# The second branch's merge gates of row pairs two and three by seven block products, with h of those rows kept transposed in DRAM

## The chip, the cores and the metric

The kernel runs on one core of one Trainium2 chip. The metric is device time in microseconds (us) of one execution. Three runs of the kernel before took 2771.01, 2769.5 and 2768.42 us, median 2769.5. One further execution was taken with the hardware profiler.

The engines are called by their short names: PE (TensorE, matmuls), DVE (VectorE), ACT (ScalarE), POOL (GpSimd) and SP (SyncE, which here only issues transfers).

## The reference

One layer of a streaming encoder, for 2048 prompt rows and 64 decode rows, all in float32, width 1024:

```python
h = rmsnorm(x, norm_g)
q, k, v, ga, u, gb, mg = split(h @ w_in)        # 1024 columns each, mg has 2048
att = stick_breaking(q, k, v)                   # 8 heads of 128, causal
pb = multi_scale_pool(u, w_pool, pool_scale)
y_a = (att * silu(ga)) @ w_br_a
y_b = (pb * silu(gb)) @ w_br_b
gate = sigmoid(mg)
m = gate[..., :1024] * y_a + gate[..., 1024:] * y_b
y = rmsnorm(x + m @ w_out, final_g)
```

The change is about the second half of `mg`, the 1024 columns of `w_in` from 7168 on, and `gate[..., 1024:]`, which I call the second branch's merge gate. k, v and the tail of u are outputs too.

## The kernel before

**Number format.** Every matmul operand is split into a rounded high part and the remainder (`split`, lines 76 to 82: ACT casts, DVE or POOL subtracts). A product is three matmuls: high by high, high by low, low by high.

**Two halves.** The 2112 rows are worked in two halves, A (1024 prompt rows and the 64 decode rows, `RA` = 1088) and B (1024 rows). For each half the transposed h is built first: rows are loaded, normalised (`normalise`, lines 197 to 205: DVE scales, POOL multiplies by the gain for the right half of the columns), transposed by PE and split into `hhi` and `hlo` (`transposed_h`, lines 207 to 214). Then come the eight attention heads with their projections, then the gates and the pooling branch.

**Direct slabs.** `proj` (lines 276 to 290) makes 128 output columns: it loads a slab of `w_in`, splits it, and runs for each column group of rows 8 k-tiles by 3 matmuls. The groups of half A are 512, 256 and 320 rows wide, those of half B 512 and 512. `merge_gate` is a slab whose result goes through a sigmoid to DRAM (`sm_d`), through one of three buffers with the tag "out" (`outgoing`), which key and value rows use as well. On half A the slabs are interleaved with the attention of the decode rows (`sample_stream`); `run` gives each generator a total time and always takes the one that is least far along, so these totals set PE's order.

**Closing stage.** y_a, y_b and m @ w_out are made by block products (Winograd's form of Strassen's scheme): rows in pairs of 352-row blocks, columns and depth in halves of 512, seven products instead of eight. A pair covers 704 rows, so three pairs cover all 2112. `order` lists the products: branch, pair t, product p. One product is 2 x 2 output tiles of 12 matmuls (`product`, lines 986 to 994), 48 matmuls of 352 columns. The weight side needs four differences of weight blocks per weight matrix (`differences`), kept in DRAM (`tw_d`): those of w_br_a and w_br_b are made by POOL (`weight_sums`) while half B's last merge gates run, those of w_out by DVE in the closing stage (`sums_step`). `forms` loads and splits a weight block, in two halves. The row side is loaded by `load_rows` from the transposed branch inputs in DRAM (`aT_d`, `bT_d`), combined by `sum3`, `sum12`, `sum4` and split by `make`, two products ahead. `emit` takes a finished block: DVE adds the kept product, multiplies by the gate, for the second branch adds the first branch's part, and POOL's queue stores it.

**What sets the order.** PE follows the program throughout. In the closing stage PE, DVE, ACT and SP all follow the program, in which `weights_at(2 * s + cc)` is called twice per product; `when` and `sums_at` say at which of these half products a weight form or a difference is made. The other engines' order before that is set by a scheduler. In all stages an engine's queue is worked in order, SP's too: a transfer that waits for its buffer holds those behind it.

## Time and profile before

| | |
|---|---|
| timed runs, median of 3 | 2769.5 us (2768.42 to 2771.01) |
| profiled execution, whole | 2771.89 us |
| its span | 2770.2 us |
| granted PE clock, mean | 0.995 |
| half A, up to the last transposes of half B's h | about 0 to 1130 us |
| half B's heads and pooling | to about 2090 us |
| half B's last 15 merge gate slabs | to 2257 us |
| first 42 block products | 2257 to about 2580 us |
| output product, residual, norm | to the end |

A profile row has the line, the engine, the operation, the names of output and input, the shape and a count, then busy time and mean duration, then the idle time of the engine just before and what ended it. Window rows have the busy time of each engine in a stretch with the number of instructions in brackets. Waits have the total, how often, and the longest. PE's matmuls overlap, so their pace is read from their starts or from a count per window and not from their durations.

### The profile page before, as it was taken

How to read it: one execution, taken by the hardware profiler on the slowest of the kernel's cores; microseconds unless marked ns; L12 is line 12 of the kernel's file. 1: busy time of each engine (PE TensorE's matmuls, PEld its weight loads, DVE VectorE, ACT ScalarE, POOL GpSimd, SP SyncE). 2: the span in 40 equal slices, each digit the busy share in tenths (PEclk: the TensorE clock that was granted, in tenths of full speed). 3: DMA queues.
4: the chain of work that ended last, by engine and by line, in shares of the span. 5: the costliest groups of instructions: out<-in, count | busy, mean ns of one | idle time of the engine just before them, and what ended most of it. 6: DMA issues, size and time to landing. Idle time of an engine off the chain costs nothing.

```text
span 2770.2 us, 41810 instructions
## 1 busy us (share of the span) xinstructions
PE 2703.7 (98%) x15052; PEld 2362.0 (85%) x15052; DVE 1833.7 (66%) x2843; ACT 1267.0 (46%) x2520; POOL 582.7 (21%) x1285
## 2 busy tenths in 40 slices
PE   6999999999999999999999999999999999999898
PEld 6988888988998989888888888887778889999786
DVE  6555555567777684487878888886452237786776
ACT  4445444455555553355555555554222223333343
POOL 2112222220000001222432343331005501110001
PEclk9999999999999999999999999999999999999999
DMA  5224222234544545311111211112337848777653
GB/s 147 79 84 131 73 72 72 77 96 152 153 155 146 157 141 153 94 46 54 54 46 50 58 54 42 51 38 84 111 100 227 268 162 275 268 258 239 219 161 118
DMA packets 344397, 343.87 MB, mean 124 GB/s; under 512 B 30062, under 2 KB 286558, under 8 KB 344188
## 3 DMA queue, kind: packets, MB, share of 16 engines
q1 hardware_dynamic: 329756, 294.26, 34.4%
q0 software_dynamic: 14432, 46.93, 4.8%
q8 instruction: 118, 1.93, 0.3%
q14 instruction: 91, 0.75, 0.1%
HBM read 232.46 MB, written 108.65 MB: 123 GB/s over the span
## 4 chain that ended last, share of the span: by engine, by line
PE 89%; DVE 5%; DMA 2%; issue 2%; ACT 1%; POOL 1%; SPq 0%; POOLq 0%; DVEq 0%; ACTq 0%
PE pj L284 17%; PE pj L285 17%; PE pj L286 17%; PE tr L638 4%; PE x L989 3%; PE x L991 3%; PE x L993 3%; PE att L655 2%; PE att L654 2%; PE z L627 2%; PE att L653 2%; PE z L626 2%; PE z L625 2%; PE y L989 2%; PE y L991 2%; PE y L993 2%
## 5 line engine op out<-in xcount | busy, mean ns | idle before, releaser
L284 PE MATMUL pj<-hhi,whi 128*128 128x512 f32 (+2 forms) x2608 | 946.3, 363 | 0.0
L286 PE MATMUL pj<-hhi,wlo 128*128 128x512 f32 (+2 forms) x2608 | 918.4, 352 | 0.0
L285 PE MATMUL pj<-hlo,whi 128*128 128x512 f32 (+2 forms) x2608 | 917.5, 352 | 0.1
L286 PEld LDWEIGHTS pj<-hhi,wlo 128*128 128x128 f32 x2608 | 492.4, 189 | 65.1
L284 PEld LDWEIGHTS pj<-hhi,whi 128*128 128x128 f32 x2608 | 495.0, 190 | 59.6 <-ACT hhi L81 0.2
L285 PEld LDWEIGHTS pj<-hlo,whi 128*128 128x128 f32 x2608 | 494.1, 189 | 59.1 <-DVE hlo L82 0.4
L579 DVE TENSOR_TENSOR_SCAN om<-om 128x513 f32<-128x513 f32 (+3 forms) x356 | 387.4, 1088 | 212.3 <-POOL om L561 108.4
L569 ACT ACTIVATE om<-z 128x512 f32<-128x512 f32 (+2 forms) x320 | 171.6, 536 | 322.1 <-PE z L627 271.6
L82 DVE TENSOR_TENSOR wlo<-raw,whi 128x512 fp32r<-128x512 f32 x248 | 176.9, 717 | 197.9 <-ACT whi L81 197.2
L581 POOL COPY carry<-om 128x1 f32<-128x1 f32 x356 | 78.6, 221 | 918.3 <-DVE om L579 877.8
L582 DVE TENSOR_TENSOR be<-be,om 128x512 f32<-128x512 f32 (+3 forms) x356 | 230.2, 647 | 31.5
L81 ACT CAST whi<-raw 128x512 fp32r<-128x512 f32 x256 | 158.3, 623 | 184.2 <-PE pj L285 167.9
L81 ACT CAST a<-tr 128x512 fp32r<-128x512 f32 (+2 forms) x356 | 188.0, 528 | 100.6 <-PE tr L638 90.0
L82 DVE TENSOR_TENSOR a<-tr,a 128x512 fp32r<-128x512 f32 (+2 forms) x356 | 215.2, 605 | 23.9 <-ACT a L81 21.9
L638 PE MATMUL tr<-ident,be 128*128 128x128 f32 x1088 | 175.6, 274 | 6.1 <-DVE be L582 3.6
L638 PEld LDWEIGHTS tr<-ident,be 128*128 128x128 f32 x1088 | 136.1, 140 | 44.6 <-DVE be L582 8.3
L570 ACT ACTIVATE be<-z 128x512 f32<-128x512 f32 (+2 forms) x320 | 170.0, 531 | 0.0
L653 PE MATMUL att<-a,v 128*128 128x512 f32 (+1 forms) x320 | 133.2, 416 | 0.0
L574 POOL COPY om<-carry 128x1 f32<-128x1 f32 x224 | 124.0, 554 | 2.7 <-DVE be L582 0.7
L561 POOL TENSOR_SCALAR_AFFINE_SELECT om<-om 128x128 f32<-128x128 f32 x128 | 50.3, 393 | 346.3 <-ACT om L569 346.1
L655 PE MATMUL att<-a,v 128*128 128x512 f32 (+1 forms) x320 | 118.4, 370 | 3.9 <-DVE a L82 3.6
L654 PE MATMUL att<-a,v 128*128 128x512 f32 (+1 forms) x320 | 117.4, 367 | 0.0
(314 smaller groups left out, 4678.7 us busy)
## 6 DMA issues: line engine op xcount, KB each, us to landing
raw<-in_w_in_dram SPq DMA_DIRECT2D x256, 256.0 KB, 3.2
sg<-sm_d SPq DMA_DIRECT2D x48, 352.0 KB, 6.1
kraw<-in_cache_k_dram SPq DMA_DIRECT2D x64, 256.0 KB, 3.4
vraw<-in_cache_v_dram SPq DMA_DIRECT2D x64, 256.0 KB, 2.9
sm_d<-sgm SPq DMA_DIRECT2D x48, 256.0 KB, 2.4
wraw<-tw_d SPq DMA_DIRECT2D x24, 512.0 KB, 4.2
out_dram<-nat SPq DMA_DIRECT2D x42, 256.0 KB, 2.3
r<-aT_d SPq DMA_DIRECT2D x12, 704.0 KB, 7.1
```

The lines of the kernel that those rows point to most:

```text
L81: nc.scalar.copy(hi, src)
L82: (nc.gpsimd if eng == "g" else nc.vector).tensor_tensor(lo, src, hi.bitcast(F32), op=ALU.subtract)
L284: nc.tensor.matmul(ps[:, 0:n], whi[:, k], hhi[:, k, c0:c0 + n], start=k == 0, stop=False)
L285: nc.tensor.matmul(ps[:, 0:n], whi[:, k], hlo[:, k, c0:c0 + n], start=False, stop=False)
L286: nc.tensor.matmul(ps[:, 0:n], wlo[:, k], hhi[:, k, c0:c0 + n], start=False, stop=k == KT - 1)
L569: nc.scalar.activation(om[:, off:512], z[:, off:512], AF.Sigmoid, scale=-SCALE)
L579: nc.vector.tensor_tensor_scan(rev, rev, rev, 1.0, op0=ALU.mult, op1=ALU.bypass)
L582: nc.vector.tensor_tensor(be[:, off:512], be[:, off:512], om[:, off + 1:513], op=ALU.mult)
L638: nc.tensor.transpose(tr[:, i * P:(i + 1) * P], be[:, off + j * P:off + (j + 1) * P], ident)
L653: nc.tensor.matmul(self.acc[:, s], vhi[:, js], ahi[:, s], start=first, stop=False)
L654: nc.tensor.matmul(self.acc[:, s], vlo[:, js], ahi[:, s], start=False, stop=False)
L655: nc.tensor.matmul(self.acc[:, s], vhi[:, js], alo[:, s], start=False, stop=last)
```

## The change

Rows 0 to 703 of the second branch's merge gate stay direct: half A's eight slabs of it run over two groups of 352 rows (`GROUPS_S`) instead of 1088 rows, interleaved with the first branch's slabs. Rows 704 to 2111 leave the direct slabs; half B's eight slabs of that gate are gone. In their place, the closing stage begins with 14 more products (branch index 0 in the new `order`, pairs t = 1 and 2), whose weights are the second half of the merge columns of `w_in` and whose rows are h itself. `emit` then applies the sigmoid on ACT and stores the gate to `sm_d`, where the second branch reads it later.

For that, h of rows from 704 on is needed transposed in DRAM (`hT_d`): `transposed_h` adds high and low part on POOL into an "out" buffer, and SP stores it. There are 24 such pieces.

The differences change hands: POOL makes those of `w_in` earlier, beside half B's pooling slabs, in the buffers of the attention's keys; those of w_br_a and w_br_b are now made by DVE during the 14 new products, from SP loads into four buffers of their own (`own`), one set every four half products. The differences of w_out come 28 half products later than before, and so does everything after the first branch's start.

```diff
+GROUPS_S = ((0, 352), (352, 352))
...
+    hT_d = dram.tile([D, R], F32, name="hT_d")
...
-        def transposed_h(i, b, m, xt):
+        def transposed_h(half, i, b, m, xt):
...
+            c0 = half * RA + i * P
+            if c0 + m > 2 * NR:
+                ht = outgoing("ht").rearrange("p (j r) -> p j r", j=4)
+                hi, lo = (t[:, b * 4:b * 4 + 4, i * P:i * P + m].bitcast(F32) for t in (hhi, hlo))
+                nc.gpsimd.tensor_tensor(ht[:, :, 0:m], hi, lo, op=ALU.add)
+                nc.sync.dma_start(hT_d[b * 512:(b + 1) * 512, c0:c0 + m].rearrange("(j p) r -> p j r", p=P),
+                                  ht[:, :, 0:m])
...
+            merges = [2 * g, KT + 2 * g, 2 * g + 1, KT + 2 * g + 1] if g < 3 else [2 * KT - 2, 2 * KT - 1]
+            merges = [proj(GROUPS_A if c < KT else GROUPS_S, [merge_gate(0, c)]) for c in merges]
+            rest.append(merges.pop(0))
             rest.append(pool_group(0, g))
-            rest += [proj(GROUPS_A, [merge_gate(0, 3 * g + i)]) for i in (1, 2)]
-        rest += [proj(GROUPS_A, [merge_gate(0, c)]) for c in range(12, 2 * KT - 2)]
-        run((sample_stream(), SAMPLE_NS), (chain(*rest), 28.0 * pns))
+            rest += merges
+        run((sample_stream(), SAMPLE_NS), (chain(*rest), 27.2 * pns))
...
+        weights = (win[:, OFF_M + D:OFF_M + 2 * D], w_br_a[0], w_br_b[0], w_out[0])
...
-                    t[nm] = kept_tile("ws").rearrange("p a b -> p (a b)")[:, 0:512]
+                    t[nm] = attp.tile([P, 512], F32, name="ws", tag="khi", bufs=4)
...
+        run((chain(*rest), 13.0), (weight_sums(0), 4.0))
...
-            yield from weight_sums(0)
-            yield from weight_sums(1)
...
-        run((chain(*[proj(GROUPS_B, [merge_gate(1, c)]) for c in range(1, 2 * KT)]), 15 * slab_ns(1)),
-            (before_closing(), 21.0))
+        run((chain(*[proj(GROUPS_B, [merge_gate(1, c)]) for c in range(1, KT)]), 7 * slab_ns(1)),
+            (before_closing(), 13.0))
...
-        order = [(i, t, p) for i in range(2) for t in range(3) for p in range(7)]
+        order = [(i, t, p) for i in range(3) for t in range(0 if i else 1, 3) for p in range(7)]
...
-            src = (aT_d, bT_d)[i]
+            src = (hT_d, aT_d, bT_d)[i]
...
-            sg = sgs_.pop(n)
             if other is not None:
                 nc.vector.tensor_tensor(other, src, other, op=ALU.add)
                 src = other
-            nc.vector.tensor_tensor(sg, src, sg, op=ALU.mult)
-            if i:
+            if i == 0:
+                sg = gates.tile([P, 2, NR], F32, name="sg", bufs=5)
+                nc.scalar.activation(sg, src, AF.Sigmoid)
+            else:
+                sg = sgs_.pop(n)
+                nc.vector.tensor_tensor(sg, src, sg, op=ALU.mult)
+            if i == 2:
                 nc.vector.tensor_tensor(sg, sg, mps.pop(n), op=ALU.add)
...
-        sums_at = {11 + 4 * k: k for k in range(4)}
+        sums_at = {39 + 4 * k: (3, k) for k in range(4)}
+        own_at = {4 * k + 4 * (i - 1) * 4: (i, k) for i in (1, 2) for k in range(4)}
+
+        def own():
+
+            spare.append(gates.tile([P, 2, NR], F32, name="ws", tag="mp" if len(spare) % 4 < 3 else "mq",
+                                    bufs=3 if len(spare) % 4 < 3 else 1))
+            return spare[-1].rearrange("p a b -> p (a b)")[:, 0:512]
```

Three places of the built order are shown. The first is ACT at the start of the closing stage: `x` are kept products, `rhi` the high part of the next row form, `r` and `s` loaded row blocks and their sums, `sg` the finished gate. Before:

```order
L1004 COPY x_24350<-x 128x704
L1004 COPY x_24377<-x 128x704
L81 CAST rhi<-r_24309 128x1408
L81 CAST rhi<-r_24307 128x1408
L1004 COPY x_24476<-x 128x704
```

And now, at the same place on ACT:

```order
L1019 COPY x_23601<-x 128x704
L1019 COPY x_23636<-x 128x704
L84 CAST rhi<-r_23566 128x1408
L1153 ACTIVATE sg<-x_23601 128x704
L1153 ACTIVATE sg<-x_23636 128x704
L84 CAST rhi<-r_23564 128x1408
L1019 COPY x_23741<-x 128x704
```

Two sigmoids of the kept and added products now stand ahead of the second cast.

The second place is DVE at the same point, `rlo` being the low part of a row form and `ws` a weight block of `own`. Before:

```order
L82 TENSOR_TENSOR rlo<-r_24309,rhi 128x1408
L1096 TENSOR_TENSOR r_24319<-r_24319,r_24309 128x1408
L1135 TENSOR_TENSOR x_24350<-y,x_24350 128x704
L1137 TENSOR_TENSOR sg<-x_24350,sg 128x704
L1135 TENSOR_TENSOR x_24377<-y,x_24377 128x704
L1137 TENSOR_TENSOR sg<-x_24377,sg 128x704
L82 TENSOR_TENSOR rlo<-r_24307,rhi 128x1408
```

And now, at the same place on DVE:

```order
L85 TENSOR_TENSOR rlo<-r_23566,rhi 128x1408
L1111 TENSOR_TENSOR r_23570<-r_23570,r_23566 128x1408
L1149 TENSOR_TENSOR x_23601<-y,x_23601 128x704
L939 TENSOR_TENSOR ws<-ws 128x512 x4
L1149 TENSOR_TENSOR x_23636<-y,x_23636 128x704
L85 TENSOR_TENSOR rlo<-r_23564,rhi 128x1408
```

The two gate multiplies are gone, and four weight differences stand between the two adds.

The third place is POOL where half B's h is built; `xb` are rows multiplied by the gain, `wlo` low parts of slab weights, `ht` the new sums for DRAM. Before:

```order
L202 TENSOR_TENSOR xb<-xb,g_bc 128x512 x5
L82 TENSOR_TENSOR wlo<-raw,whi 128x512 x2
L202 TENSOR_TENSOR xb<-xb,g_bc 128x512
L82 TENSOR_TENSOR wlo<-raw,whi 128x512 x2
L202 TENSOR_TENSOR xb<-xb,g_bc 128x512 x2
```

And now, at the same place on POOL:

```order
L205 TENSOR_TENSOR xb<-xb,g_bc 128x512 x3
L221 TENSOR_TENSOR ht<-hhi,hlo 128x512 x3
L205 TENSOR_TENSOR xb<-xb,g_bc 128x512
L221 TENSOR_TENSOR ht<-hhi,hlo 128x512 x3
L85 TENSOR_TENSOR wlo<-raw,whi 128x512 x2
L205 TENSOR_TENSOR xb<-xb,g_bc 128x512
L221 TENSOR_TENSOR ht<-hhi,hlo 128x512
L205 TENSOR_TENSOR xb<-xb,g_bc 128x512
L221 TENSOR_TENSOR ht<-hhi,hlo 128x512
L85 TENSOR_TENSOR wlo<-raw,whi 128x512 x2
```

Six sums now stand ahead of the fifth multiply, and the first pair of weight splits has moved ahead of it.

83 lines of the change are left out of this document (44 added, 39 removed).

## The prediction

> **What bounds the kernel now.** I read the page first, then the busy time by stage, then the waits of TensorE (PE), and only then single rows.
>
> ```profile
> span 2770.2 us, 41810 instructions
> PE 2703.7 (98%) x15052; PEld 2362.0 (85%) x15052; DVE 1833.7 (66%) x2843; ACT 1267.0 (46%) x2520; POOL 582.7 (21%) x1285
> 2100.00:2200.00 100.00, 100.00 (x430) 80.48 (x429) 23.83 (x22) 23.02 (x40) 63.09 (x80) 1.00 0.80 251
> 2257.00:2400.00 143.00, 140.70 (x882) 140.11 (x883) 95.89 (x88) 47.54 (x47) 21.70 (x34) 1.00 0.80 269
> 2400.00:2500.00 100.00, 100.00 (x631) 100.00 (x631) 78.12 (x70) 34.01 (x33) 11.45 (x16) 1.00 0.82 272
> PE x L989 <- DVE sg L1137: 2.0, 2, 1.0
> PE x L991 <- DVE rlo L82: 1.2, 1, 1.2
> ```
>
> In a window row the brackets count instructions, and the last three numbers are granted clock, busy share of the transfer engines and GB/s. PE is busy 98% of the span and both stages that the change edits are full: the direct slabs at 2100 to 2200, and the block products that I call the closing stage, from 2257. The last two rows are all the waits of PE there that are put down to VectorE (DVE). So what PE no longer has to do leaves the span, unless a feeder becomes late. The same rows give PE's pace: 100 us / 430 = 232.6 ns for a 512-column matmul, 100 / 631 = 158.5 ns for a 352-column one. The two shorter direct groups come from first and last rows, ten gaps each: 1.19 / 10 = 119 ns and 1.47 / 10 = 147 ns.
>
> ```profile
> 1092.60 0.28 PE L285 MATMUL pj<-hlo,whi 128*128 128x256 f32 x1
> 1093.79 0.29 PE L286 MATMUL pj<-hhi,wlo 128*128 128x256 f32 x1
> 1102.48 0.31 PE L285 MATMUL pj<-hlo,whi 128*128 128x320 f32 x1
> 1103.95 0.31 PE L286 MATMUL pj<-hhi,wlo 128*128 128x320 f32 x1
> ```
>
> **PE work, removed and added.** A direct slab is 24 matmuls per column group. The second branch's eight slabs cost, on the first half, 8 x 24 x (0.2326 + 0.119 + 0.147) = 95.7 us, on the second 8 x 48 x 0.2326 = 89.3 us; together 185.0 us go. What comes: eight slabs of two 352-column groups, 8 x 48 x 0.1585 = 60.9 us, and 14 block products of 48 matmuls, 14 x 48 x 0.1585 = 106.5 us; together 167.4 us. Net -17.6 us. That is less than a seventh because the first 704 rows stay direct. By the Trainium skill (TensorE: Matmul & The Clock Gate, "Wait — 56ns, not 53.3ns?") warm matmuls start N / 2.4 GHz plus about 2.5 ns apart; the same counts would then make 171.3 removed, 157.5 added, net -13.8. The trace's 232.6 ns against that rule's 215.8 disagrees, and I keep -17.6.
>
> **Closing stage, the first pair of blocks.** For the new pairs the gate is not multiplied by DVE; ScalarE (ACT) takes the sigmoid after DVE has added. ACT's cast of the next rows (L84) stands behind both sigmoids in ACT's queue, where before it stood behind nothing of the emission, and DVE has four weight differences between the two adds.
>
> ```profile
> 2272.36 1.62 DVE L82 TENSOR_TENSOR rlo<-r,rhi 128x1408 fp32r<-128x1408 f32 x1 [1.44 <-ACT rhi L81]
> 2273.90 1.61 DVE L1096 TENSOR_TENSOR r<-r,r 128x1408 f32<-128x1408 f32 x1
> 2275.43 0.88 DVE L1135 TENSOR_TENSOR x<-y,x 128x704 f32<-128x704 f32 x1
> 2276.35 0.89 DVE L1137 TENSOR_TENSOR sg<-x,sg 128x704 f32<-128x704 f32 x1
> 2278.89 1.62 DVE L82 TENSOR_TENSOR rlo<-r,rhi 128x1408 fp32r<-128x1408 f32 x1
> 2319.81 2.87 DVE L922 TENSOR_TENSOR wraw<-wraw 128x512 f32<-128x512 f32 x4
> L81 ACT CAST rhi<-r 128x1408 fp32r<-128x1408 f32 x34 | 46.7, 1375 | 103.6 <-PE y L993 46.1 <-PE x L993 46.0 <-DVE sg L1139 6.3
> L1004 ACT COPY x<-x 128x704 f32<-128x704 f32 x24 | 17.9, 747 | 61.2 <-PE x L993 61.2
> L989 PE MATMUL y<-rhi,t1hi x96: 322/322/323, 2281.6 to 2557.0; 128*128 128x352 f32 x96
> ```
>
> On the clock of before: first add done at 2276.3, four differences (2.87) 2279.2, second add (0.88) 2280.1, sigmoid at the price of ACT's copy of the same 704 columns (0.75) 2280.8, cast (1.375) 2282.2, subtract (1.62) 2283.8. PE started that product (t1, p = 3) at 2281.6 and its second matmul, which reads the subtract's result, 0.16 later. So about 2 us late: +2.0. Later pairs have the same chain, but there the row sums run a step earlier; adding up the second pair's list in order leaves it about a microsecond early. Bounds: 0 (the sigmoid may be quicker) to 2.0 twice.
>
> **Closing stage, transfers.** This is the term that decides. The sizes stand in the transfer view of 2300 to 2380, the densest 80 us of the stage before:
>
> ```profile
> DMA packets 11641, 24.01 MB, mean 300 GB/s; under 512 B 970, under 2 KB 7842, under 8 KB 11635
> sg<-sm_d SPq DMA_DIRECT2D x13, 352.0 KB, 5.9
> r<-aT_d SPq DMA_DIRECT2D x6, 704.0 KB, 7.2
> wraw<-in_w_out_dram SPq DMA_DIRECT2D x8, 512.0 KB, 5.2
> tw_d<-wraw POOLq DMA_DIRECT2D x16, 256.0 KB, 4.0
> 2314.00:2317.80 3.80, 3.80 (x26) 3.80 (x25) 2.55 (x2) 0.75 (x1) 0.23 (x1) 1.00 1.05 399
> 2367.20:2371.00 3.80, 3.80 (x26) 3.80 (x25) 3.77 (x4) 0.22 (x1) 1.08 (x2) 1.00 1.04 410
> 2470.00:2485.20 15.20, 15.20 (x98) 15.20 (x97) 11.97 (x11) 4.14 (x4) 1.43 (x2) 1.00 0.91 332
> ```
>
> In the new 106.5 us the queues carry 12 row blocks of 704 KB, 16 gate stores and 3 gate loads of 352 KB, seven sets of four 256 KB loads and four such stores for the differences of w_br_a and w_br_b (which GpSimd, POOL, made under the direct slabs before), and 16 halves of weight forms of 512 KB: 37,664 KB = 38.6 MB, or 362 GB/s. Before, 300 GB/s passed in 80 us with about 1 us of PE wait, and single 3.8 us windows moved 399 and 410 GB/s with PE full, so 362 is no wall, but leaves little. What a late transfer does: SyncE (SP) issues in order, so row blocks queue behind the difference loads that wait for their buffers; DVE's differences wait for the loads, and behind them its subtract for PE. Lower bound 0 (all inside the lookahead of one product, 7.6 us), upper bound: at 332 GB/s, the best share under 0.95, 38.6 MB take 116.3 us, +9.8. The nearest row is the 300 GB/s stretch; I take +2.0. The Trainium skill (DMA: Bandwidth & Descriptors, "Specifications") gives about 358 GB/s as what one core gets from HBM; by that alone the stage would take 107.8 us, +1.3. Its limit as a ceiling is contradicted by the 399 and 410.
>
> **h kept transposed.** POOL gets 24 adds of hi + lo, and SP 24 stores.
>
> ```profile
> 43.76 0.09 POOL L572 MEMSET om<- 128x1 f32 x1
> 90.31 0.76 POOL L561 TENSOR_SCALAR_AFFINE_SELECT om<-om 128x128 f32<-128x128 f32 x1 [46.46 <-ACT om L569]
> 1104.39 1.82 POOL L202 TENSOR_TENSOR xb<-xb,g_bc 128x512 f32<-128x512 f32 x1 [4.81 <-DVE xb L201]
> 1106.15 2.73 POOL L82 TENSOR_TENSOR wlo<-raw,whi 128x512 fp32r<-128x512 f32 x2
> 1108.86 1.29 POOL L202 TENSOR_TENSOR xb<-xb,g_bc 128x512 f32<-128x512 f32 x1
> 1104.96 0.68 DVE L82 TENSOR_TENSOR hlo<-tr,hhi 128x512 fp32r<-128x512 f32 x1
> 1110.22 0.60 PE L211 MATMUL tr<-ident,xb 128*128 128x128 f32 x4
> PE tr L211 <- DVE hlo L82: 3.5, 1, 3.5
> ```
>
> A two-input 128x512 add costs POOL 1.3 to 1.8 us. In the first half all eight stand behind the last gain multiply, in 46 us in which POOL waits; what is left is that they share three output buffers with the key and value rows, and ACT waits for such a buffer: +0.5 (0 to 3). In the second half sixteen are strewn among the multiplies (xb) and the weight splits (wlo). The multiply of 1104.39 then has six adds and two splits ahead. The sixth add reads the low part that DVE ended at 1105.6; add 1.4, splits 2.7, multiply 1.3 make 1111.0 instead of 1106.2, and PE's transpose that reads it ran at 1110.2. The next transpose already waited 3.5 us for something else, and most of the shift lies under that: +1.0 (0 to 5).
>
> **Filler for the decode stream.** On the first half the interleaved slabs shrink by 8 x (24 x 0.4986 - 48 x 0.1585) = 34.9 us, and they are spread as 27.2 slabs when they are worth about 25.2, so they run out first: the last decode block's transposes and products stand almost alone in PE's order. Its chain on ACT and DVE (sigmoids, scan, multiply) has to be awaited once: +1.0 (0 to 4).
>
> **Nothing counted.** POOL's 16 remaining differences (w_in) and their 32 transfers go under the 13 slabs before: POOL was busy 63 of 100 us for twice that work, so at most 40 us under 13 x 11.16 = 145 us. The last 7 direct slabs (78 us) must cover 12 loads with their splits: two buffers at 5 to 7 us make about 45 us. If either cover failed, the stage would open with one late load, some 5 us.
>
> **Sum.** -17.6 + 2.0 + 2.0 + 0.5 + 1.0 + 1.0 = -11.1 us. The profiled execution took 2771.9 us (span 2770.2 and 1.7 around it), so 2760.8 there; it lies 2.4 above the median of 2769.5, and a timed run should show 2769.5 - 11.1 = 2758.4.
>
> **Rivals.** First, everything added is covered: only the 17.6 counts, 2752. For it: DVE at 78% and a share of 1.05 without PE idle. Against it: the 2 us in ACT's queue order. Second, the transfers give back most: the stage runs at 332 GB/s, +9.8 in place of +2.0, net -3.3, 2766, within 0.2%. For it: 362 wanted against 300 shown over any long stretch. Against it: two of a pair's four row blocks are asked for 5 and 7 half products (3.8 us each, so 19 and 27 us) ahead, only the other two 8 to 11 us. Here the Trainium skill's 358 belongs, on the forecast's side of this. Third, on the other side: the ring of the four difference buffers is too slow.
>
> ```profile
> 2324.15 2.15 SPq L916 DMA_DIRECT2D wraw<-in_w_out_dram  x2
> 2334.31 0.54 POOL L923 DMA_DIRECT2D tw_d<-wraw  x1 [0.18 <-issue]
> 2338.85 1.57 SPq L916 DMA_DIRECT2D wraw<-in_w_out_dram  x2
> ```
>
> Load, subtract, store, load again took 2338.85 - 2324.15 = 14.7 us before, where a round has two products, 15.2 us. If landings stretch so that it takes 18.5, seven rounds add 23 us, in place of the 2.0: net +10, 2780. It decides from 15.2 + 13.1 / 7 = 17.1 us up. For it: 0.5 us of margin. Against it: 14.7 holds part of the stage's own pacing, and four separate buffers let stores start after the first difference. Fourth, the change could not do what it says; the built order shows the 14 products and the 352-column groups, so I give that nothing.
>
> **How the numbers follow.** Within 0.2% (5.5 us) a measurement can't be told from no change; faster means under 2764.0. Forecast 2758.4 with its terms' bounds (2754 to 2764): 0.50. All covered (2752 to 2754): 0.15. Transfers give back most (2764 to 2771): 0.22. Ring too slow: 0.13. Faster 0.65, same 0.21, slower 0.14. The range leaves out the ring's time and the very edge below: 2752 to 2771.
>
> **What would show it.** Right: busy PE about 17 us less; the first new product p = 3 waits about 2 us for L85's rlo, put down to ACT's cast; the new 106 us at over 340 GB/s with PE idle under 6 us. Wrong: waits of PE on DVE's L939 differences or SP's row blocks that recur every 15 us (transfers or ring); a wait near 1110 to 1120 that grows beyond 5 us (POOL); 352-column matmuls of a direct slab that start other than 158 ns apart.

## The result, and the profile after

Four runs of the changed kernel took 2803.81 to 2813.17 us, median 2809.2; four of the kernel before, on the same chip, had a median of 2770.0. The ratio is 1.0135 (95% interval 1.0123 to 1.0147): by this ratio the change makes the kernel slower by 37 us (39 between the medians), where 11 us less was forecast. The profiled execution is the fastest of the four, 2803.8 us, 31.9 above the profiled one of before; all readings below compare these two. The times of all kernels are medians over their fast runs.

The page of the kernel after, span and busy time:

```profile
span 2802.1 us, 42288 instructions
PE 2701.5 (96%) x15148; PEld 2379.9 (85%) x15148; DVE 1909.4 (68%) x2907; ACT 1296.4 (46%) x2536; POOL 602.4 (21%) x1309
```

PE should have been busy for 2703.7 - 17.6 = 2686.1 us. It was busy for 2701.5, and idle for 100.6 where it had been idle for 66.5. So the gain was more than lost in two ways: 34.1 us more idle, and 15.4 us in which the same matmuls took longer; 34.1 + 15.4 - 17.6 = 31.9. The second part fits the clock: its mean over the span went from 0.995 to 0.990, and 1.0% of 2802.1 less 0.5% of 2770.2 is 14 us. Where the clock falls is seen in windows of the kernel after, about one product long (after PE's, PEld's, DVE's, ACT's and POOL's busy time come granted clock, share of the transfer engines, GB/s):

```profile
2199.00:2206.40 7.40, 6.34 (x38) 5.76 (x36) 5.11 (x6) 3.59 (x4) 1.92 (x3) 1.00 0.98 343
2206.40:2214.00 7.60, 5.25 (x18) 5.25 (x19) 5.45 (x6) 2.20 (x3) 2.39 (x4) 0.56 1.02 360
2214.00:2221.60 7.60, 7.60 (x49) 7.60 (x48) 2.44 (x3) 2.62 (x3) 1.43 (x2) 1.00 0.78 247
2305.20:2312.80 7.60, 2.23 (x8) 2.24 (x9) 7.53 (x8) 1.76 (x2) 2.11 (x4) 0.57 0.82 270
2312.80:2320.40 7.60, 7.60 (x39) 7.60 (x39) 1.51 (x2) 0.75 (x1) 0.00 (x0) 0.76 0.98 338
2153.00:2290.00 137.00, 125.80 (x745) 122.69 (x746) 81.58 (x77) 54.56 (x60) 26.80 (x44) 0.96 0.81 281
```

In the second row PE starts 18 matmuls where the third row has 49: 3.4 us of stops with the end of the first row, and after them a clock of 0.56. The two rows together start 56 matmuls where 95 would fit at 158 ns, so 3.4 us of stops cost about 6. The fifth row has no stop at all and still only 39, after the long stop of the row before. If all slower matmuls follow stops as these do, the stops cost almost half as much again after they end, 15.4 us for 34.1. The Trainium skill (TensorE: Matmul & The Clock Gate, "What's actually happening") says that PE falls to half its clock after about 3.4 us without work and needs about as long at work to get it back. These rows agree on the half clock, with matmuls 0.29 us apart in place of 0.16. They differ in the times: the longest single stop ahead of the clock of 0.56 is 2.85 us, and the slow pace lasted 5.2 us from there (2208.7 to 2213.9).

To find the places I compare four landmarks: the transposes of half B's h (xb), the closing stage's first matmul, and the first cast of the output product (rhi<-mt), which ends the stretch that I call the closing stage below. Rows of before:

```profile
L211 PE MATMUL tr<-ident,xb x64: 270/272/477, 1092.0 to 1127.4; 128*128 128x128 f32 x64
L989 PE MATMUL x<-rhi,b11hi x96: 322/323/397, 2257.0 to 2534.1; 128*128 128x352 f32 x96
L81 ACT CAST rhi<-mt x9: 408/622/626, 2577.2 to 2739.8; 128x512 fp32r<-128x512 f32 x8, 128x256 fp32r<-128x256 f32 x1
```

The same of after:

```profile
L214 PE MATMUL tr<-ident,xb x64: 270/273/474, 1065.2 to 1106.2; 128*128 128x128 f32 x64
L1004 PE MATMUL x<-rhi,b11hi x128: 322/322/427, 2153.2 to 2566.7; 128*128 128x352 f32 x128
L84 ACT CAST rhi<-mt x9: 407/622/624, 2610.6 to 2774.6; 128x512 fp32r<-128x512 f32 x8, 128x256 fp32r<-128x256 f32 x1
```

| stretch | before | should be | after | lost |
|---|---|---|---|---|
| up to the last xb transpose | 1127.4 | 1127.4 - 34.9 = 1092.5 | 1106.2 | 13.7 |
| from there to the closing stage | 1129.6 | - 89.3 = 1040.3 | 1047.0 | 6.7 |
| closing stage | 320.2 | + 106.5 = 426.7 | 457.4 | 30.7 |
| to the end of the span | 193.0 | 193.0 | 191.5 | -1.5 |

The four losses make 49.6, the 31.9 and the 17.6 that should have been gained. What PE waits for at the head of the closing stage, 2145 to 2420, in the kernel after (total, how often, longest):

```profile
PE y L1006 <- DVE rlo L85: 9.0, 3, 6.5
PE x L1006 <- DVE rlo L85: 4.4, 3, 1.9
PE x L1008 <- DVE t4lo L963: 2.8, 1, 2.8
```

And DVE and SP there:

```profile
DVE rlo L85 <- ACT rhi L84: 48.5, 18, 8.8
DVE ws L939 <- DMA ws<-in_w_br_b_dram: 11.7, 7, 3.5
DVE ws L939 <- DMA ws<-in_w_br_a_dram: 2.7, 2, 1.4
SPq L935 <- DMA tw_d<-ws: 29.1, 7, 13.8
SPq L956 <- DVE t2lo L963: 16.5, 2, 8.6
SPq L956 <- DVE t1lo L963: 15.7, 2, 13.6
```

PE has two waits put down to VectorE at this place in before, 2.2 us; now it waits 16.2 us for the subtracts of rows (rlo) and weights (t4lo), DVE stands 14.4 us at differences (ws) whose loads have not landed, and SP 29.1 us at loads whose buffers are not yet stored. That gave the theory for the experiments: DVE's queue, which holds PE's subtracts behind differences that wait for transfers. Its rival is the transfers' bandwidth alone.

The longest stop shows the theory in one chain of the changed kernel, DVE's rows first and PE's wait last (start, duration, and in brackets the idle time before):

```profile
2301.52 0.69 DVE L939 TENSOR_TENSOR ws<-ws 128x512 f32<-128x512 f32 x1 [2.19 <-DMA ws<-in_w_br_b_dram]
2303.97 2.15 DVE L939 TENSOR_TENSOR ws<-ws 128x512 f32<-128x512 f32 x3 [1.76 <-DMA ws<-in_w_br_b_dram]
2306.03 1.22 DVE L963 TENSOR_TENSOR t3lo<-wraw,t3hi 128x1024 fp32r<-128x1024 f32 x1
2307.17 0.88 DVE L1149 TENSOR_TENSOR x<-y,x 128x704 f32<-128x704 f32 x1
2308.08 0.89 DVE L1156 TENSOR_TENSOR sg<-x,sg 128x704 f32<-128x704 f32 x1
2308.89 1.61 DVE L85 TENSOR_TENSOR rlo<-r,rhi 128x1408 fp32r<-128x1408 f32 x1
2310.57 0.66 PE L1006 MATMUL y<-rlo,t1hi 128*128 128x352 f32 x1 [6.54 <-DVE rlo L85]
```

From 2299.3 to 2306.1 four differences hold DVE for 6.8 us, 2.8 of work and 4.0 of waiting for two loads. The rows' subtract, whose cast was done at 2299.3, stands behind them, and PE stops for 6.5 us. SP had issued these loads only at 2295.0: it had stood at the loads of weight forms (L956), up to 13.6 us, for a buffer that DVE's own subtract of a weight frees. The same holds for most of DVE's waits: 11.7 of the 14.4 us are at loads of w_br_b, which had at most 0.5 us of SP's waits for the ring's own buffers ahead of them.

### The profile page after: what moved, and what is told of

Its sections match the earlier page's. It is cut to its first block, busy times and chain, and to the rows that moved or that the text cites. A ratio compares the mean times of both kernels' runs of the same rounds, so it can differ in the third digit from the quotient of the medians.

```text
span 2802.1 us, 42288 instructions
## 1 busy us (share of the span) xinstructions
PE 2701.5 (96%) x15148; PEld 2379.9 (85%) x15148; DVE 1909.4 (68%) x2907; ACT 1296.4 (46%) x2536; POOL 602.4 (21%) x1309
## 4 chain that ended last, share of the span: by engine, by line
PE 77%; DVE 7%; issue 6%; DMA 5%; POOL 2%; ACT 2%; SPq 0%; POOLq 0%; DVEq 0%; ACTq 0%
PE pj L294 14%; PE pj L295 14%; PE pj L296 14%; PE tr L648 4%; PE att L665 2%; PE x L1004 2%; PE x L1006 2%; PE x L1008 2%; PE z L637 2%; PE z L636 2%; PE att L664 2%; PE z L635 2%; PE att L663 2%; PE y L1006 2%; PE y L1004 2%
## 5 line engine op out<-in xcount | busy, mean ns | idle before, releaser
L294 PE MATMUL pj<-hhi,whi 128*128 128x512 f32 (+3 forms) x2416 | 874.2, 362 | 0.0
L296 PE MATMUL pj<-hhi,wlo 128*128 128x512 f32 (+3 forms) x2416 | 847.1, 351 | 4.3 <-POOL wlo L85 4.3
L295 PE MATMUL pj<-hlo,whi 128*128 128x512 f32 (+3 forms) x2416 | 845.8, 350 | 0.1
L296 PEld LDWEIGHTS pj<-hhi,wlo 128*128 128x128 f32 x2416 | 456.8, 189 | 61.3 <-POOL wlo L85 4.7
L294 PEld LDWEIGHTS pj<-hhi,whi 128*128 128x128 f32 x2416 | 459.3, 190 | 51.5 <-ACT hhi L84 0.2
L295 PEld LDWEIGHTS pj<-hlo,whi 128*128 128x128 f32 x2416 | 458.5, 190 | 51.1 <-DVE hlo L85 0.4
L85 DVE TENSOR_TENSOR wlo<-raw,whi 128x512 fp32r<-128x512 f32 x232 | 161.9, 701 | 129.1 <-ACT whi L84 127.8
L84 ACT CAST whi<-raw 128x512 fp32r<-128x512 f32 x240 | 148.4, 623 | 148.3 <-PE pj L295 133.4
L663 PE MATMUL att<-a,v 128*128 128x512 f32 (+1 forms) x320 | 133.2, 416 | 0.0
L665 PE MATMUL att<-a,v 128*128 128x512 f32 (+1 forms) x320 | 118.6, 371 | 4.0 <-DVE a L85 3.7
L84 ACT CAST rhi<-r 128x1408 fp32r<-128x1408 f32 x46 | 63.0, 1370 | 123.9 <-PE y L1008 49.3
```

The lines of the kernel that those rows point to most:

```text
L84: nc.scalar.copy(hi, src)
L85: (nc.gpsimd if eng == "g" else nc.vector).tensor_tensor(lo, src, hi.bitcast(F32), op=ALU.subtract)
L294: nc.tensor.matmul(ps[:, 0:n], whi[:, k], hhi[:, k, c0:c0 + n], start=k == 0, stop=False)
L295: nc.tensor.matmul(ps[:, 0:n], whi[:, k], hlo[:, k, c0:c0 + n], start=False, stop=False)
L296: nc.tensor.matmul(ps[:, 0:n], wlo[:, k], hhi[:, k, c0:c0 + n], start=False, stop=k == KT - 1)
L663: nc.tensor.matmul(self.acc[:, s], vhi[:, js], ahi[:, s], start=first, stop=False)
```

## The experiments: the closing stage

All ratios are to the kernel before, timed beside it. The closing stage of ten kernels that have the stage as changed measured 454.3 to 460.9 us; only what leaves that range says something.

**Cast first.** ACT's cast and DVE's subtract of the rows after next are put ahead of the second half's add and sigmoid:

```diff
+                early = i == 0 and cc == 1 and p in (1, 4, 5, 6)
...
                 out = acc[:, :, 0:NR]
+                if early:
+                    make(s + 2)
...
-                    make(s + 2)
+                    if not early:
+                        make(s + 2)
```

> The changed kernel, but for the second branch's two block pairs the cast and subtract that make the rows of the product after next stand ahead of the gate's add and sigmoid of the second column half, on both ACT and DVE. Theory (feeders: the closing stage lost 30.7 us, about half of it because ACT's cast waits for DVE's add and then for the sigmoid, 2.1 us of gap on DVE each time, and the lowered clock after such stops makes it more): the first 14 products' 18 us of PE waits on rlo fall to under 6, the closing stage goes from 457 us to 443 (438 to 448), the whole from 2807 to 2793. Rival (transfers alone: 38 MB asked for in 106 us): nothing that is moved changes a byte, so the stage stays within 3 us of 457 and the whole within 3 of 2807.

Measured: 2804.0 us, ratio 1.0114 (1.0099 to 1.0130); closing stage 454.2. The stage is at the lower edge of its range, so alone the edit's effect is too small to tell, and the expected 14 us did not come. The waits moved:

```profile
PE y L1006 <- DVE rlo L85: 6.8, 1, 6.8
PE x L1004 <- ACT sg L1153: 5.7, 2, 4.1
PE x L1008 <- DVE t4lo L963: 2.2, 1, 2.2
```

PE now waits 5.7 us that are put down to ACT's sigmoid instead.

**POOL makes the differences.** Those of w_br_a and w_br_b go back to POOL, under the direct slabs, so the closing stage has no ring:

```diff
-        run((chain(*rest), 13.0), (weight_sums(0), 4.0))
+        run((chain(*rest), 13.0), (chain(pause(1.0), weight_sums(0), weight_sums(1)), 9.0))
...
+            yield from weight_sums(2, lambda: kept_tile("ws").rearrange("p a b -> p (a b)")[:, 0:512])
             yield from forms(0, ("b11", "b21", "t1", "t2"), True)
...
-        own_at = {4 * k + 4 * (i - 1) * 4: (i, k) for i in (1, 2) for k in range(4)}
+        own_at = {}
```

> The changed kernel, but the differences of w_br_a and w_br_b are made by POOL under the direct slabs, so that the closing stage's first 14 products have no ring of loads, differences and stores. Theory (feeders): the 28 differences (20 us of DVE), DVE's 14 us of waits on their loads and SP's 29 us of waits on their buffers go; the cast behind the sigmoid stays; closing stage from 457 us to 440 (435 to 446); some of it may be lost under the slabs before, where POOL already holds up SP by 16 us. Rival (transfers alone): with 14 MB fewer in the stage nothing is late any more and the stage takes its 427 us of matmuls, all 30 us back. Second rival (the sigmoid's place in ACT's queue alone): stage stays above 452.

Measured: 2785.7 us, 1.0048 (1.0035 to 1.0060); the closing stage runs from 2157.1 to 2590.4, 433.3 us. That is 24 us less, a little more than the theory's 17, and 6.6 short of the rival's 427. To separate the ring's two sides, two kernels keep one each. (The ring has eight sets of four differences, 32 in all; the eighth falls in the first branch's first products.)

**Transfers without differences.** The ring loads and stores the same bytes, DVE does nothing to them:

```diff
                 for j, out, x, y in differences(t):
-                    nc.vector.tensor_tensor(out, x, y, op=ALU.subtract)
+                    if own is None:
+                        nc.vector.tensor_tensor(out, x, y, op=ALU.subtract)
```

> The changed kernel without the 28 differences of w_br_a and w_br_b on DVE: their blocks are loaded into the ring and stored again as they are, at the same places, so every byte stays (it leaves these differences out of what is computed). The ring cost 24 us of the closing stage (457 to 433 without it). Theory (DVE: its queue stands still at a difference until its load lands, and the subtract that PE needs stands behind it): with no difference in DVE's queue the stage falls to 437 (433 to 443), though the transfers are all there. Rival (the transfers themselves: bytes beside the row blocks and forms make those land late, and SP's queue stops at the ring's buffers): stage stays above 450.

**Differences without transfers.**

```diff
-                        nc.sync.dma_start(b, weights[i][r:r + P, j * 512:(j + 1) * 512])
+                        nc.gpsimd.memset(b, 0.0)
...
-                    nc.gpsimd.dma_start(tw_d[i, j, k * P:(k + 1) * P, :], out)
+                    if own is None:
+                        nc.gpsimd.dma_start(tw_d[i, j, k * P:(k + 1) * P, :], out)
...
-                src = tw_d[i, int(nm[1]) - 1]
+                src = tw_d[0 if i in (1, 2) else i, int(nm[1]) - 1]
```

> The changed kernel with the 28 differences on DVE, on buffers that are set to zero in place of being loaded, and with no stores of them; the forms of these two weights read the stored differences of w_in (it leaves the true differences out of what is computed). So DVE's time and places stay, the ring's 14 MB go. Theory (DVE waits for loads in its queue): the waits go with the loads, and what is left is DVE's 20 us of differences, mostly in its gaps: stage 438 to 444. If DVE's mere time is the cause: above 450. Rival (transfers): stage 433 to 436, as with all of the ring gone.

Measured: 2788.5 us without differences, 1.0057 (1.0042 to 1.0072), and 2795.1 without transfers, 1.0079 (1.0064 to 1.0095). Their stages:

| | transfers | no transfers |
|---|---|---|
| differences | 457.4 (454.3 to 460.9) | 441.0 |
| no differences | 438.6 | 433.3 (with cast first added 430.1 to 437.4 in five kernels below) |

Rows of the kernel without differences, the stage's start and end and its first 133 us:

```profile
L1005 PE MATMUL x<-rhi,b11hi x128: 320/322/400, 2157.1 to 2552.6; 128*128 128x352 f32 x128
L84 ACT CAST rhi<-mt x9: 407/621/622, 2595.7 to 2760.3; 128x512 fp32r<-128x512 f32 x8, 128x256 fp32r<-128x256 f32 x1
2157.00:2290.00 133.00, 126.62 (x771) 124.56 (x772) 69.54 (x54) 56.14 (x60) 26.78 (x44) 0.99 0.83 293
```

Every byte is still moved, at 293 GB/s where the changed kernel had 281, and PE is idle for 6.4 us in 133 where it was idle for 11.2 in 137. So bandwidth alone is not the bound. Taking the differences alone away gives back 18.8 of the 24.1 us, the transfers alone 16.4: 35 for two parts of 24. In the ratios it is the same, 0.78% and 0.56% for parts of 0.87%. Seen from the other end, DVE's 22 us of differences cost 7.7 by themselves and the transfers 5.3; the other 11 (a rough size, with 3 to 4 us of scatter in each cell) come from their meeting: a difference in DVE's queue that waits for its load, with PE's subtract behind it.

The whole stage in the four kernels (as changed, differences alone, transfers alone, neither):

```profile
2153.20:2610.60 457.40, 436.20 (x2674) 431.94 (x2675) 316.99 (x292) 161.32 (x162) 69.91 (x109) 0.98 0.77 261
2156.90:2597.90 441.00, 430.97 (x2664) 428.14 (x2665) 316.38 (x292) 161.74 (x163) 68.50 (x109) 0.99 0.69 233
2157.10:2595.70 438.60, 431.30 (x2665) 428.90 (x2666) 296.56 (x261) 161.70 (x163) 70.02 (x109) 1.00 0.80 273
2157.10:2590.40 433.30, 428.61 (x2669) 426.63 (x2670) 295.45 (x260) 161.50 (x163) 52.34 (x77) 1.00 0.70 237
```

PE is idle in it for 21.2, 10.0, 7.3 and 4.7 us. Of the 11 us, 8.6 are therefore waits that only the two together make, and 2.5 are slower matmuls. Neither kernel is a clean half: without differences a buffer of the ring comes free sooner (SP's wait there falls from 29.1 to 14.7 us), and without transfers POOL sets the buffers to zero. A ring with more buffers, or loads issued earlier, was not tried.

## The experiments: where h is built

**Adds later.** Half B's 16 adds with their stores are collected and issued under the attention (`keep_h` holds the removed lines):

```diff
+                if half:
+                    late_h.append((i, b, m, c0))
+                else:
+                    keep_h(i, b, m, c0)
...
+            (keep_late(), 16.0))
```

> The changed kernel, but the second half's 16 adds of hi + lo on POOL, with their stores, come after the half's transposes, under the attention, in place of among them. Theory: POOL's place between the gain multiplies and the weight splits cost about 8 of the 13.6 us lost until the last h transpose; the wait of PE on POOL's wlo goes; whole 2807 to 2799 (2795 to 2803). Rival (the loss is the decode stream that outlives its shorter filler, DVE full at 1000 to 1030): within 2 us of 2807.

**Other spread.** `27.2 * pns` becomes `25.2 * pns`.

> The changed kernel, but the slabs beside the decode stream are spread as 25.2 slabs in place of 27.2, which is what they are worth with 352-column groups. Theory: the decode stream's tail no longer stands nearly alone; about 4 us of the 13.6 come back, whole 2803 (2799 to 2807). Rival (DVE itself is full there, so another spread moves the wait and does not remove it): within 2 us of 2807, or a microsecond or two slower.

**From PSUM.** ACT copies the transposes' tile instead of POOL's add:

```diff
-                hi, lo = (t[:, b * 4:b * 4 + 4, i * P:i * P + m].bitcast(F32) for t in (hhi, hlo))
-                nc.gpsimd.tensor_tensor(ht[:, :, 0:m], hi, lo, op=ALU.add)
+                nc.scalar.copy(ht[:, :, 0:m], trv[:, :, 0:m])
```

> The changed kernel, but the rows of h that are kept come from the transposes' own PSUM tile by an ACT copy, in place of POOL's add of hi + lo; the stores stay. Theory (POOL's 16 adds among the second half's gain multiplies cost about 7 us there, and the same adds moved under the attention cost it there again): the last transpose of h falls from 1106 to 1099 and, as POOL then does not have the adds anywhere, the gain lasts to the end: whole 2807 to 2800 (2797 to 2803). Rival (the end of the decode stream and the stores set it): within 3 us of 2807.

**h not kept.** The whole block after `split` in `transposed_h` is left out; `hT_d` becomes `aT_d` in `load_rows` and `before_closing`.

> The changed kernel without the 24 adds and stores of h's rows; the closing stage loads the rows of the attention's output in their place, as many bytes (it leaves h out of the second branch's gate of these rows). It prices the keeping of h. Theory (the adds and stores cost 5 to 8 us in the stretch where the second half's h is built, and moving them to another engine or another stretch moved that cost along): last transpose of h at 1106 - 7 = 1099, whole 2800 (2797 to 2803). Rival (the loss there belongs to the decode stream alone): within 2 us of 2807.

**Full groups.** `GROUPS_A if c < KT else GROUPS_S` becomes `GROUPS_A`, and the spread 28.0.

> The changed kernel, but the second branch's eight direct slabs of the first half take all three column groups again (what they make too much is made again later), with the spread of before: 34.9 us more of matmuls beside the decode stream. Theory (part of the first half's gain was lost since the decode stream, with DVE full at its end, outlives its shorter filler): the last transpose of h goes from 1106 to 1106 + 35 - 6 = 1135, whole 2836 (2833 to 2839). Rival (the loss is all due to keeping h): 1141, whole 2842.

**Stores by POOL.** `nc.sync.dma_start(hT_d` becomes `nc.gpsimd.dma_start(hT_d`.

> The changed kernel, but the 24 stores of h's rows are issued by POOL, right behind its adds, and no longer stand in SP's queue. Theory (SP issues in order; it stood 24 us at stores that waited for POOL's adds, and loads of x and of slab weights behind them came late): most of the 11 us that keeping h costs come back, last transpose of h 1108 to 1099, whole 2807 to 2798 (2795 to 2802). Rival (POOL's adds among the gain multiplies): within 3 us of 2807.

**No add.** The store's source is `hhi[:, b * 4:b * 4 + 4, i * P:i * P + m]`; add and buffer go.

> The changed kernel without POOL's 24 adds and without the buffers that they write: SP stores the high part of h as it lies (it leaves the low part out of these rows). Stores, bytes and SP's places stay. Theory (SP's wait for the adds): a store then waits only for ACT's cast, so it holds SP up less; last transpose of h 1108 to 1100, whole 2798. Rival (bytes and places of the stores themselves): within 3 us of 2807.

**No store.** The add stays, the `nc.sync.dma_start(hT_d` goes, and the loads read `aT_d`.

> The changed kernel with POOL's 24 adds, but with no stores of h's rows; the closing stage loads the attention's output in their place (it leaves h out of these rows' gate). Theory (SP's queue): as fast as with neither, last transpose of h 1097 to 1099, whole 2791 to 2797. Rival (POOL's adds in the way of multiplies and splits): 1104 or later, whole 2802 or above.

| kernel | time us | ratio (95%) | xb transposes, first to last us | length |
|---|---|---|---|---|
| before | | 1 | 1092.0 to 1127.4 | 35.4 |
| as changed | 2809.2 | 1.0135 (1.0123 to 1.0147) | 1065.2 to 1106.2 | 41.0 |
| adds later | 2805.7 | 1.0122 (1.0108 to 1.0136) | 1066.3 to 1098.7 | 32.4 |
| other spread | 2805.2 | 1.0113 (1.0097 to 1.0129) | 1062.2 to 1103.1 | 40.9 |
| from PSUM | 2805.9 | 1.0122 (1.0107 to 1.0137) | 1069.6 to 1105.9 | 36.3 |
| h not kept | 2791.5 | 1.0071 (1.0058 to 1.0085) | 1064.9 to 1097.2 | 32.3 |
| full groups | 2829.5 | 1.0206 (1.0190 to 1.0221) | 1094.8 to 1136.5 | 41.7 |
| stores by POOL | 2820.1 | 1.0174 (1.0160 to 1.0188) | 1071.4 to 1118.2 | 46.8 |
| no add | 2798.2 | 1.0097 (1.0081 to 1.0112) | 1064.5 to 1097.1 | 32.6 |
| no store | 2798.1 | 1.0093 (1.0079 to 1.0108) | 1068.4 to 1104.5 | 36.1 |

The length column is the cleanest measure: nine kernels with this part as changed have 40.6 to 42.1. Stores without adds (no add) are as short as nothing at all, 32.6 against 32.3: the stores' bytes and their places in SP's queue cost nothing in this stretch. Adds without stores lengthen it by 3.8, adds with stores by 8.7. What the stores add to the adds stays open between two causes. One is SP, which stands at stores that wait for POOL's adds, with loads behind them; from 1060 to 1112 in the kernel after:

```profile
SPq L222 <- POOL ht L221: 23.7, 15, 3.9
```

The other is the three shared buffers, which a store holds longer: ACT waits 4.3 us there for stores of h to leave one. The kernel with POOL's stores takes them off SP and still got slower, but it puts another load on POOL (last section), so it does not refute the first. To keep h costs 9 us in this stretch, 8.7 up to the closing stage's start (2144.5 in place of 2153.2), 13.4 between the profiled spans (2788.7, 2802.1) and 0.64%, about 18 us, between the medians. Put under the attention, the adds cost it there: its stretch, from the last xb transpose to the last attention transpose, took 796.1 us with the adds later, 789.8 as changed and 788.1 before. So neither moving the adds, nor another engine, nor another spread gave the 4 to 8 us that were expected of each. ACT's copies make the stretch 4.7 shorter than the adds do, but the whole not measurably.

How DVE fares beside the adds shows in two groups, from 1060 to 1112 in the kernel after and 1088 to 1132 before (busy, mean ns, idle before). First after:

```profile
L204 DVE TENSOR_SCALAR xb<-xb,rstd 128x512 f32<-128x512 f32 x5 | 4.9, 970 | 2.3 <-POOL ht L221 1.5 <-DMA xb<-in_x_prompt_dram 0.8
L85 DVE TENSOR_TENSOR klo<-kst,khi 128x256 fp32r<-128x256 f32 x3 | 3.2, 1071 | 0.1
L85 DVE TENSOR_TENSOR hlo<-tr,hhi 128x512 fp32r<-128x512 f32 x16 | 11.0, 685 | 17.6 <-ACT hhi L84 17.6
L221 POOL TENSOR_TENSOR ht<-hhi,hlo 128x512 f32<-128x512 f32 x16 | 21.8, 1370 | 17.8 <-DMA sm_d<-sgm 9.8 <-DVE hlo L85 6.9 <-DMA hT_d<-ht 1.0
```

Then before:

```profile
L201 DVE TENSOR_SCALAR xb<-xb,rstd 128x512 f32<-128x512 f32 x5 | 2.7, 542 | 1.4 <-DMA xb<-in_x_prompt_dram 1.4
L82 DVE TENSOR_TENSOR klo<-kst,khi 128x256 fp32r<-128x256 f32 x2 | 0.8, 418 | 0.0
L82 DVE TENSOR_TENSOR hlo<-tr,hhi 128x512 fp32r<-128x512 f32 x16 | 10.9, 688 | 18.6 <-ACT hhi L81 18.6
```

DVE's own instructions get slower beside POOL's adds: the row scaling from 542 to 970 ns, the key's subtract from 418 to 1071, while the subtract that reads PSUM keeps its 685. From 1050 to 1115 the row scaling's mean is 782 to 992 ns in nine kernels with adds and stores as changed, 711 with adds and no stores, and 523 to 670 in seven kernels without POOL's adds there. The Trainium skill (SBUF — State Buffer, "Who interferes with whom") says that POOL shares a pair of SBUF ports with DVE, and that a DVE instruction with two SBUF inputs, or in a mode that takes both ports, contends with it. The key's subtract, with two SBUF inputs, and the subtract that reads PSUM agree; whether the row scaling runs in such a mode no row shows. What this costs PE was not separated by a run from POOL's order, in which an add stands ahead of a weight split that PE waits for:

```profile
1090.31 0.39 PE L296 MATMUL pj<-hhi,wlo 128*128 128x256 f32 x1 [3.30 <-POOL wlo L85]
```

Full groups put 34.9 us of matmuls back beside the decode stream, yet the last xb transpose moves by 30.3 us (27 to 30 from the 1106.2 to 1109.2 of six kernels with this part as changed), the span by 28.4 (2830.5, 2802.1) and the whole by 0.71%, 20 us, between the medians. So 5 us or more of the first half's gain were lost. The likely reason is that the decode stream outlives its shorter filler: at its end, in the kernel after, DVE is full and PE is not:

```profile
1020.00:1040.00 20.00, 16.80 (x114) 15.91 (x113) 19.67 (x57) 11.39 (x27) 0.76 (x3) 1.00 0.53 163
```

The other spread moves the last transpose by 3 us; its whole time can't be told from the changed kernel's, as the intervals overlap.

## The experiments: after the attention, and sums

**Products first.** POOL's loads of w_in are pinned behind what stands before them, so that the last attention output's multiply (ao) comes first, and they start later in the interleaving:

```diff
-                    nc.gpsimd.dma_start(t[nm], weights[i][r * 512 + k * P:r * 512 + (k + 1) * P, c * 512:(c + 1) * 512])
+                    tc.keep_in_program_order(nc.gpsimd.dma_start(t[nm], weights[i][r * 512 + k * P:r * 512 + (k + 1) * P, c * 512:(c + 1) * 512]))
...
-        run((chain(*rest), 13.0), (weight_sums(0), 4.0))
...
+        run((chain(*rest), 13.0), (chain(pause(3.0), weight_sums(0)), 7.0))
```

> The changed kernel, but on POOL the loads and differences of w_in come behind the last attention output's gate multiply (ao) in POOL's order, in place of ahead of it. Theory: SP's store of ao no longer holds up SP for 16 us, the slab weights behind it arrive in time, and the 5.3 us lost between the last attention transpose and the last pooling product come back: whole 2807 to 2802 (2800 to 2804). Rival (the pooling transposes wait for DVE, not for SP): within 2 us of 2807. If the differences then end too late for the first forms of the closing stage, its start is later by some 5 us: 2812.

Measured: 2803.7, 1.0116 (1.0099 to 1.0132). SP's wait in the kernel after, 1895 to 1925:

```profile
SPq L671 <- POOL ao L669: 16.0, 1, 16.0
```

and in this one:

```profile
SPq L671 <- POOL ao L669: 2.9, 1, 2.9
```

The wait of SP goes as expected; from the last attention transpose to the closing stage it is 254.8 us against 257.2, with 252.2 due. That does not show that the wait cost anything: twelve kernels without this edit and without more differences on POOL, the changed one among them, have 254.8 to 258.2, and the 254.8 is that of POOL's stores, in which SP waits 16.1 us for ao. What PE itself waits for in the stretch is the pooling's history rows (hist), 3.8 us as changed, 2.9 in this kernel and nothing before; what makes them late stays open.

**Together.** Cast first, POOL's differences, products first and the other spread:

> The changed kernel with four of the edits together: casts first in the new products, the differences of w_br_a and w_br_b on POOL before the closing stage, all of POOL's differences behind the last attention output in POOL's order, and the 25.2 spread. Theory (the parts are separate): closing stage 430 us (428 to 434) against 433 with the differences gone alone, the stage starts 3 to 6 us earlier than there, whole 2807 - 25 - 3 - 4 - 2 = 2773 (2769 to 2779), so no faster than the kernel before (2772). If POOL can't make 48 differences behind the attention in time, the stage starts late by 5 us or more and the whole is 2780 or above.

The same with h from PSUM and the old spread:

> As the kernel with the edits together, without the 25.2 spread and with h's rows copied from PSUM by ACT in place of POOL's adds. Theory (POOL is free for the multiplies, but the cost of keeping h moves to ACT): within 4 us of the other, 2774 (2769 to 2780). Rival (with POOL also charged with 32 more differences, freeing it pays): 5 us or more under it.

Cast first, POOL's differences, POOL's stores, other spread:

> The changed kernel with casts first in the new products, the differences of w_br_a and w_br_b on POOL before the closing stage (in the order that the scheduler chooses), h's stores issued by POOL and the 25.2 spread. Theory: of the 32 us that the change lost beside its 17.6 us gain, 27 come back in the closing stage, 9 where h is built, 3 in the decode stream: 2807 - 39 = 2768 (2764 to 2776), at most a tie with the kernel before (2772). If POOL's stores there get in the way of its multiplies, 2778 or above.

Measured: 2781.5, 1.0041 (1.0027 to 1.0054); 2785.4, 1.0046 (1.0033 to 1.0059); 2791.6, 1.0072 (1.0059 to 1.0085). The first two have closing stages of 430.1 and 431.3, the third 433.5, against 433.3 without cast first: what the cast's place is worth is within the scatter even with the ring gone. The first two pay ahead of the stage: with 48 differences pinned behind ao, PE waits for the pooling's history rows, in the first of them

```profile
PE tr L412 <- DVE hist L371: 8.5, 4, 3.5
```

where it was 3.8 us as changed, and 263 us pass from the attention's end to the stage where 257 did. The third carries POOL's stores, with a stretch of 46.3 us; alone they made the kernel 11 us slower.

**Low part later.** A full kernel without adds: SP stores hhi, POOL issues accumulating transfers of hlo later, pinned, beside the decode stream and the last direct slabs; with cast first, POOL's differences, other spread:

```diff
+                nc.sync.dma_start(rows(), hi)
+                late_h.append(lambda: nc.gpsimd.dma_start(rows(), lo, accum_op=ALU.add))
```

> A full kernel again: h's rows without any add by POOL and without the shared buffers. SP stores the high part as it lies, and POOL issues transfers that add the low part to it in DRAM later, beside the decode stream and behind the attention; with it the casts first, the differences of w_br_a and w_br_b on POOL before the closing stage and the 25.2 spread. Theory (POOL's adds and the buffers cost 9 to 11 us, the ring 26, the cast's place 2 to 3): last transpose of h 1094 to 1098, closing stage 430, whole 2807 - 41 = 2766 (2762 to 2774), for the first time not slower than the kernel before (2772). If the adding transfers cost POOL as much as its stores did (10 us with those), 2776 or above.

**Sum check.** The same without the accumulating transfers; it leaves the low part of h out of the kept rows.

> The same without the low part of h (it leaves it out of the kept rows): the sum of all causes found, with nothing in place of the adds. Theory (the causes are all of the loss but the pooling transposes' 5 us and 2 to 3 us in the decode stream): 2764 (2760 to 2770), under the kernel before by some 8 us of the 17.6 that the matmul count gives. If something not found is left, 2775 or above.

Measured: 2780.8, 1.0033 (1.0021 to 1.0046), and 2772.2, 1.0001 (0.9992 to 1.0010). No full kernel of this form beat the kernel before. With the low part's transfers the gain of the stretch (32.7) is gone again behind the attention: 267.1 us pass there to the stage where 257.2 did, and PE waits longer for history rows, and SP for ao:

```profile
L231 POOL DMA_DIRECT2D hT_d<-hlo x24: 1267/1362/1907, 46.2 to 2011.4; - x24
SPq L679 <- POOL ao L677: 21.8, 1, 21.8
PE tr L420 <- DVE hist L379: 11.9, 4, 8.2
```

The sum check takes 37 us off the changed kernel and ends level with the kernel before, where 2764 was expected. By its profiled run (2775.4 us) it is 21.1 us above the 2752.6 us span that before's 2770.2 less 17.6 would be: 5.3 up to the last xb transpose, 2.0 in the attention, 4.3 from there to the closing stage, 10.7 in the stage (437.4), and -1.1 at the end. Of the stage's 10.7, most lies in its first 61 us, which start 153 + 179 matmuls where full slices have 193 or 194, 55 fewer at 157 ns, 8.6 us:

```profile
2144.40:2174.90 30.50, 27.50 (x153) 26.97 (x154) 11.27 (x8) 7.52 (x9) 1.45 (x2) 0.89 0.55 186
2174.90:2205.40 30.50, 28.91 (x179) 28.28 (x178) 18.41 (x15) 15.68 (x17) 3.56 (x5) 1.00 0.66 218
2205.40:2235.90 30.50, 30.50 (x193) 30.50 (x192) 16.99 (x13) 14.83 (x16) 2.15 (x3) 1.00 0.34 109
```

Before has 182 in its first slice and 194 in its second. Why this stage opens slowly even without the ring stays open, as do the 4 us between the attention and the stage.

## Why the prediction was wrong, point by point

- **PE's work, -17.6: right.** A full 30.5 us slice starts 193 or 194 block matmuls, 157 to 158 ns apart, and in the best of six kernels without the ring the stage comes to 430.1 against the 426.7 of the count. The forecast that busy PE falls by 17 was wrong all the same (2.2): it left out that lost time slows the matmuls after it.
- **Closing stage, transfers, +2.0 (0 to 9.8): the step that failed.** It named the mechanism, differences that wait for their loads with PE's subtract behind them, but priced it by bandwidth alone, 38.6 MB at 332 GB/s at worst. Bandwidth was not the limit (293 GB/s passed with PE idle for 6.4 of 133 us); waiting in DVE's queue was, and with the clock that follows a stop the ring cost 24 us (17 to 31 with the scatter of both stages). The lookahead of one product that its lower bound of 0 rests on did not hold: SP issued the loads late, as in the chain above.
- **Ring too slow: the nearest rival, by place and sign, and by luck in size.** Sets of differences follow each other on DVE every 18.4 us (2173.0 to 2301.5, seven rounds) where 15.2 were planned, and its price of 23 us is about what the ring cost. But its mechanism, a round of load, subtract and store that is itself too long, fits only the early sets: the loads at which DVE waited most were issued right after SP had stood at other loads. Either part of the ring taken away gives back over two thirds.
- **First pair, +2.0 (0 to 4): not settled.** The foreseen wait is there but shorter: the product named, t1 with p = 3, waits 1.2 us for rlo in the first pair, and 1.5 in the second, which was to be early. Putting the cast first moved neither time nor stage by more than their scatter.
- **h kept, +1.5 (0 to 8): wrong by a factor of six to twelve.** It counted one add's delay at one transpose. Adds alone lengthen the stretch by 3.8 us, and with their stores by 8.7; how much of it is DVE's slowing, POOL's order, SP's waits or the buffers was not separated. No single wait of PE there grew beyond the 5 us of its sign: the longest is 3.3.
- **Filler, +1.0 (0 to 4): too small**, about 5 or more.
- **"Nothing counted": 5.0 us were lost between the attention and the stage.** The 145 us of slabs cover POOL's work, but it stands ahead of ao in POOL's queue and holds SP for 16 us; that this cost PE time is not shown, and the cause stays open.

## What to carry to other kernels

Price an operation moved onto an in-order queue by what stands behind it when its input is late, and not by its own length or by bytes: differences and their transfers cost 8 and 5 us apart and 24 together here. On a kernel whose PE is 98% busy, count a stop of 3 us as 5 or more, for the matmuls after it run slower. Do not count work that fills another chain's waits as saved in full: of 34.9 us taken from beside the decode stream, 5 or more did not come back.

## What the runs showed of the hardware

A store of a piece of h that POOL issues keeps POOL for 0.75 to 0.95 us, and a transfer that adds such a piece to what stands in DRAM for 1.27 to 1.91 us, where the store of a difference took 0.54. The first costs more than half an add:

```profile
L222 POOL DMA_DIRECT2D hT_d<-ht x24: 750/767/950, 46.7 to 1122.6; - x24
```

For half B's 16 that is 12 us of POOL in a stretch of 41. It fits the 11 us by which moving the stores off SP made the kernel slower: the stretch grew by 5.8 us, and the first attention product starts at 93.1 us in place of 89.3.
